# Banded-attention scores as two 64-row matmuls on the two halves of the partitions

## The chip, the cores and the metric

The kernel runs on one core of one Trainium2 chip. The metric is the device time of one execution in microseconds (us), as the median of several runs. The engines carry their usual names in the profile: PE is TensorE (the matrix engine), PEld its loading of weights, DVE is VectorE, ACT is ScalarE, POOL is GpSimd, SP is the engine that issues the transfers.

## The reference

Two layers of a hybrid decoder trunk on 256 tokens with 2048 channels. Each layer has a mixer (three groups of heads side by side: gated linear attention, banded attention with sinks, a short convolution), a cross-attention into 256 memory tokens, and a gated feed-forward part. The part that the change touches is the banded attention: 16 query heads of 64 channels share 2 key heads, a query sees the 128 last positions, and the tokens are cut into two blocks of 128:

```python
def swa_with_sinks(q, k, v, sinks):
    B, T, Hq, hd = q.shape
    ...
    kk, vv = with_prev(k), with_prev(vf)
    s = jnp.einsum('bnqhgd,bnkhd->bnhgqk', qb, kk) * (hd ** -0.5)
    ...
    s = jnp.where(valid[None, :, None, None], s, -jnp.inf)
    ...
    m = jnp.maximum(jnp.max(s, axis=-1, keepdims=True), sink)
    p = jnp.exp(s - m)
    denom = jnp.sum(p, axis=-1, keepdims=True) + jnp.exp(sink - m)
    o = jnp.einsum('bnhgqk,bnkhd->bnqhgd', p / denom, vv)
    return o.reshape(B, T, Hq * hd)
```

The change concerns the first einsum, s.

## The kernel before

All weights are streamed once from memory in pieces of 128 by 1024 (`stream`, L158 to L161): ScalarE casts a piece to the rounded number format fp32r (`wh`), VectorE subtracts to get the rest (`wl`), and every product is made of three matmuls, high by high, high by low and low by high. The large products (`xstat`, L193 to L195, and `wstat`, L176 to L180) give the stream of matmuls; behind each of their steps, `pump` lets one of the waiting tasks go on (the linear attention, the banded attention, the turning of outputs), so that the small matmuls of those tasks stand between the large ones. Three buffers of `wh` and `wl` are in turn. The order of each engine's instructions is not that of the source alone: a scheduler of the framework plans all instructions on a modelled timeline and may move them against each other; `high_priority` moves the weights' casts ahead.

PSUM has eight banks of 512 columns. Four belong to the large products; four are shared by all small products (`self.bank`).

In the banded attention the query heads are stored in pairs: a transposed tile `qT` holds head j of the first key head on partitions 0 to 63 and head j of the second on 64 to 127. `swa_keys` (L597 to L613) turns the rotated keys into `kp`, of shape [128, 2 heads, 2 (high, low), 256]; rows 0 to 63 are filled for head 0 and rows 64 to 127 for head 1, and the other halves are zero (the memset at L600). So one matmul over all 128 rows gives the scores of both heads side by side (L649), one head adding zeros to the other's. `swa` (L634 on) runs for each of two groups g of four head pairs and two blocks n of 128 queries: block 0 has 128 keys (`kw`), block 1 has 256. A bank `sc` holds two head pairs for block 0 and one for block 1; for each pair there are three matmuls (high and low), then one read by VectorE for each head, which adds the mask and takes the maximum (L652), and then the task yields. Over two layers these are 48 score matmuls of 256 columns and 48 of 512.

The early part of a layer that the prediction also speaks of: `zkq` is the projection of the linear attention's keys and queries (wstat), `zq` the one of the banded attention's queries (xstat), `kq` the scaled copy of the first (L714), and `gla` then forms exponents of the gates, `e` and `kd`, on VectorE (L471, L472, L506). L490, L522 and L536 are the linear attention's own products of 64 rows.

Of the kernel before, what the change touches and what calls it, by code (L numbers as in the profile page):

```python
# [9 lines left out]
F32 = mybir.dt.float32  # L10
F32R = mybir.dt.float32r
# [6 lines left out]
P = 128  # L18
D = 2048
T = 256  # L20
# [52 lines left out]
class Trunk:  # L73
# [522 lines left out]

    def swa_keys(self, tok, kp, vp):  # L597

        nc = self.nc
        nc.gpsimd.memset(kp.bitcast(F32), 0.0)  # L600
        nc.gpsimd.memset(vp.bitcast(F32), 0.0)
        kr = self.t512("kr")
        for tb in range(2):
            self.rope(kr[:, tb * P:(tb + 1) * P], tok[tb][:, 16:16 + P], (1.0, -1.0), tb, 2)
        yield W["kr"]
        pk = self.bank("kT")
        for tb in range(2):
            nc.tensor.transpose(out=pk[:, tb * P:(tb + 1) * P], in_=kr[:, tb * P:(tb + 1) * P], identity=self.ident)
        for h in range(2):
            rows, cs = slice(h * 64, h * 64 + 64), slice(h * 64, h * 64 + 64)  # L610
            self.split(kp[rows, h, 0, :], kp[rows, h, 1, :], pk[rows, 0:T])
            for tb in range(2):
                self.split(vp[:, tb, h, 0, cs], vp[:, tb, h, 1, cs], tok[tb][:, 144 + h * 64:208 + h * 64])  # L613

# [19 lines left out]
    def swa(self, g, n, qTs, kp, vp, out):  # L634

        nc = self.nc
        hs = slice(4 * g, 4 * g + 4)
        qT = qTs[n]
        c = self.cols("swc", 32)
        mx, nm, dn, es = (c[:, 8 * i:8 * i + 8].rearrange("p (j h) -> p j h", h=2) for i in range(4))  # L640
        kw = P * (n + 1)
        per = 2 - n
        probs = []
        for j0 in range(0, 4, per):
            sp = self.bank("sc", (P, per, 2, kw))
            pr = self.t512("pr", (P, per, 2, kw))
            for i in range(per):
                for m, (u, v) in enumerate(((0, 0), (0, 1), (1, 0))):
                    nc.tensor.matmul(sp[:, i], lhsT=qT[:, u, j0 + i, :], rhs=kp[:, :, v, 0:kw],  # L649
                                     start=(m == 0), stop=(m == 2))  # L650
                for h in range(2):
                    nc.vector.tensor_tensor_reduce(pr[:, i, h, :], sp[:, i, h, :], self.mask[:, T - kw:T],  # L652
                                                   1.0, -3e38, ALU.add, ALU.max,
                                                   accum_out=mx[:, j0 + i, h:h + 1])
                yield 1
            probs.append(pr)
        nc.vector.scalar_tensor_tensor(nm, mx, -1.0, self.nsink[:, hs, :], ALU.mult, ALU.min)
        nc.vector.tensor_tensor(es, nm, self.nsink[:, hs, :], ALU.subtract)
        for j in range(4):
            for h in range(2):  # L660
                p = probs[j // per][:, j % per, h, :]
                nc.scalar.activation(p, p, AF.Exp, bias=nm[:, j, h:h + 1], accum_out=dn[:, j, h:h + 1])
        nc.scalar.activation(es, es, AF.Exp)
        nc.vector.tensor_tensor(dn, dn, es, ALU.add)
        nc.vector.reciprocal(dn, dn)
        for j in range(4):
            for h in range(2):
                p = probs[j // per][:, j % per, h, :]
                nc.vector.tensor_scalar(p, p, dn[:, j, h:h + 1], None, ALU.mult)
        yield W["p"]  # L670
        ov = self.bank("ov", (P, 4, P))
        parts = [(h, kb) for h in range(2) for kb in range(n + 1)]
        for h, kb in parts:
            pt = self.bank("pT", (P, 4, P))
            for j in range(4):
                nc.tensor.transpose(out=pt[:, j, :], in_=probs[j // per][:, j % per, h, kb * P:(kb + 1) * P],
                                    identity=self.ident)
            pT = self.actp.tile([P, 2, 4, P], F32R, tag="act", name="pT")
            self.split(pT[:, 0], pT[:, 1], pt)
            yield W["pT"]  # L680
            for u, v in ((0, 0), (1, 0), (0, 1)):
                nc.tensor.matmul(ov, lhsT=vp[:, kb, h, u, :], rhs=pT[:, v],
                                 start=((h, kb) == parts[0] and u == v), stop=((h, kb) == parts[-1] and v == 1))
        if not out:
            out += [self.operand(f"ob{2 * g + i}") for i in range(2)]
        for i in range(2):
            ts = slice(n * P, (n + 1) * P)
            self.split(out[i][:, :, 0, ts], out[i][:, :, 1, ts], ov[:, 2 * i:2 * i + 2, :])


    def mixer(self, l, xs, ss, after):
        nc, a = self.nc, self.a
        tok = [self.big(f"tok{tb}", [P, 2 * TOKC]) for tb in range(2)]
        rc, rbc, rt = self.row_factor(ss, "rx", W["ss1"] if l else 1, after)
        pst = self.xstat_both(xs, a["w_tok"][l], name="tokp")
        self.layer_rest(l)
        self.until(rt)
        with self.tc.high_priority(offset=WPRIO):
            for c in range(2):
                for tb in range(2):  # L700
                    nc.scalar.activation(tok[tb][:, c * TOKC:(c + 1) * TOKC], pst[c][tb], AF.Copy,
                                         scale=rc[:, tb:tb + 1])
        qsc = self.par.tile([P, 4], F32, tag="qs", name="qs")
        nc.vector.tensor_scalar(qsc[:, 0:2], rc, 0.125, None, ALU.mult)
        nc.vector.tensor_scalar(qsc[:, 2:4], rc, -0.125, None, ALU.mult)
        fm = lambda g, name: self.fold(self.wstat(xs, a["w_fm"][l, g], name=name), name)
        kq, o_sb = self.big("kq", [P, 2, 512]), self.big("o", [P, 4, T])
        ready = []
        tg = self.start(self.gla(l, tok, kq, ready, o_sb))
        if l == 0:  # L710
            self.rope_tables()
        for g in range(2):
            z = fm(g, "zkq")
            nc.vector.tensor_tensor(kq[:, g, :].rearrange("p (h t) -> p h t", h=2), z,  # L714
                                    rbc.unsqueeze(1).broadcast_to([P, 2, T]), ALU.mult)
        nc.scalar.mul(kq[:, 1, :], kq[:, 1, :], 0.125)
        ready.append(True)
        kp, vp = self.operand("kp"), self.actp.tile([P, 2, 2, 2, P], F32R, tag="act", name="vp")
        tk = self.start(self.swa_keys(tok, kp, vp))
        ob, ts = [], []  # L720
        q = [self.big("q", (P, 2, 512)) for _ in range(2)]
        self.claim(*q)
        for g in range(2):
            qs, qTs = self.swa_rope(q[g], self.xstat(xs, a["w_q"][l, g], name="zq"), qsc), []
            og = []
            ob.append(og)
            tq = self.start(self.swa_queries(qs, qTs))
            ts += [self.start(self.swa(g, n, qTs, kp, vp, og), tk, tq) for n in range(2)]
        if l == 0:
            self.tm = self.start(self.memory_factor())  # L730
        ys, oc = self.big("cy", [P, 4, T]), [self.operand(f"oc{g}") for g in range(2)]
        self.claim(ys, *oc)
        for j in range(4):
            z = fm(4 + j, "zc")
            self.by_row(z, rbc)
            self.conv(j, z[:, 0, :], z[:, 1, :], ys[:, j, :])
        ms = []
        self.start(self.memory(l, ms), *ts)
        for g in range(2):
            z = fm(8 + g, "zb")  # L740
            self.by_row(z, rbc)
            nc.vector.tensor_tensor(z, z, ys[:, 2 * g:2 * g + 2, :], ALU.mult)
            self.split(oc[g][:, :, 0, :], oc[g][:, :, 1, :], z)
        zr, oa = self.big("zr", [P, 2, 2, T]), [self.operand(f"oa{g}") for g in range(2)]
        for g in range(2):
            z = self.fold(self.wstat(xs, a["w_fm"][l, 2 + g], name="zr"), "zr", zr[:, g])
            self.by_row(z, rbc)
        ts.append(self.start(self.gla_out(o_sb, zr, oa), tg, *ts))
        return oc + oa, ob, ts, ms
# [405 lines left out]
```

## Time and profile before

| | us |
|---|---|
| median of 3 runs | 2846.16 (2844.40 to 2846.78) |
| the profiled execution | 2846.51 |
| its span, first to last instruction | 2844.7 |
| TensorE busy | 2825.5 (99%) |
| TensorE's weight loads | 2363.4 (83%) |
| VectorE busy | 1885.5 (66%) |
| ScalarE busy | 1445.7 (51%) |
| GpSimd busy | 15.8 (1%) |

A busy share of TensorE counts overlapping work: a matmul's duration reaches from its start to its modelled end, and the next one starts before that. What a matmul takes of the engine's time is the distance from its start to the next start, as the timeline shows it. A form such as 64\*128 in a row gives the rows and the columns of the array that the matmul uses.

### The profile page before, as it was taken

Reading aid. Unit: us, or ns where it says so; the run is one execution under the profiler, and the core shown is the slowest. Engines: PE = TensorE matmul, PEld = TensorE weight load, DVE = VectorE, ACT = ScalarE, POOL = GpSimd, SP = SyncE. Lnnn points to the kernel's source line nnn. Section 1 sums busy time; section 2 is a strip of 40 time slices with the busy share of each in tenths; the row PEclk is TensorE's granted clock in tenths of the full one; section 3 lists DMA queues with packets and bytes.
Section 4 is the critical chain, followed back from the end, with each engine's and each line's share of the span. In section 5 each row is a group of like instructions: output and inputs, shape, how many; then the busy total and the mean of one; then the engine's idle time right before and its main releaser. Section 6 shows DMA issues by size and latency. Waiting matters only on the chain.

```text
span 2844.7 us, 37041 instructions
## 1 busy us (share of the span) xinstructions
PE 2825.5 (99%) x13554; PEld 2363.4 (83%) x13554; DVE 1885.5 (66%) x2877; ACT 1445.7 (51%) x2060; POOL 15.8 (1%) x44
## 2 busy tenths in 40 slices
PE   9999999999999999999999999999999999999998
PEld 8888888888888888888888888888888888888886
DVE  6886665556777777755567866655567777777445
ACT  7565454445555555544465644544455555555333
POOL 0000000000000000000000000000000000000001
PEclk9999999999999999999999999999999999999999
DMA  6557777557777777766664577775677777777665
GB/s 240 156 175 225 237 243 230 178 171 239 246 239 238 244 242 238 246 209 208 205 194 142 161 227 242 239 221 176 185 238 241 246 245 236 240 242 247 197 193 155
DMA packets 207030, 616.97 MB, mean 217 GB/s; under 512 B 23520, under 2 KB 65024, under 8 KB 206848
## 3 DMA queue, kind: packets, MB, share of 16 engines
q1 hardware_dynamic: 206848, 614.61, 68.9%
q8 instruction: 106, 1.74, 0.3%
q14 instruction: 76, 0.62, 0.1%
HBM read 570.48 MB, written 44.04 MB: 216 GB/s over the span
## 4 chain that ended last, share of the span: by engine, by line
PE 98%; DVE 1%; DMA 1%; ACT 0%; issue 0%; SPq 0%; ACTq 0%
PE up L194 11%; PE up L195 11%; PE up L193 11%; PE fin L821 8%; PE res L195 7%; PE res L193 7%; PE res L194 7%; PE qp L194 2%; PE vp L193 2%; PE vp L195 2%; PE vp L194 2%; PE qp L193 2%; PE qp L195 2%; PE kp L195 2%; PE kp L193 2%; PE kp L194 2%
## 5 line engine op out<-in xcount | busy, mean ns | idle before, releaser
L161 DVE TENSOR_TENSOR wl<-raw,wh 128x1024 fp32r<-128x1024 f32 (+1 forms) x992 | 1201.1, 1212 | 780.3 <-ACT wh L160 778.5
L160 ACT CAST wh<-raw 128x1024 fp32r<-128x1024 f32 (+1 forms) x992 | 1035.5, 1045 | 1140.7 <-PE up L195 329.8
L194 PE MATMUL up<-wl,xs 128*128 128x512 f32 x1408 | 548.1, 389 | 0.0
L193 PE MATMUL up<-wh,xs 128*128 128x512 f32 x1408 | 547.8, 389 | 0.0
L195 PE MATMUL up<-wh,xs 128*128 128x512 f32 x1408 | 547.7, 389 | 0.0
L194 PEld LDWEIGHTS up<-wl,xs 128*128 128x128 f32 x1408 | 264.3, 188 | 55.3 <-DVE wl L161 0.4
L193 PEld LDWEIGHTS up<-wh,xs 128*128 128x128 f32 x1408 | 264.3, 188 | 55.0
L195 PEld LDWEIGHTS up<-wh,xs 128*128 128x128 f32 x1408 | 264.3, 188 | 54.5
L821 PE MATMUL fin<-wh,a 128*128 128x512 f32 x704 | 189.9, 389 | 0.0
L821 PEld LDWEIGHTS fin<-wh,a 128*128 128x128 f32 x704 | 132.2, 188 | 27.5
L193 PE MATMUL res<-wh,a 128*128 128x512 f32 x352 | 136.9, 389 | 0.0
L194 PE MATMUL res<-wl,a 128*128 128x512 f32 x352 | 136.9, 389 | 0.0
L195 PE MATMUL res<-wh,a 128*128 128x512 f32 x352 | 136.9, 389 | 0.0
L1017 ACT ACTIVATE u<-z_t,par 128x256 f32<-128x256 f32 x176 | 91.5, 591 | 36.5 <-DVE z_t L238 36.3
L821 PE MATMUL fin<-wl,a 128*128 128x512 f32 x352 | 110.0, 389 | 0.0
L193 PE MATMUL vp<-wh,ms 128*128 128x512 f32 x256 | 100.3, 392 | 0.0
L193 PE MATMUL qp<-wh,xs 128*128 128x512 f32 x256 | 100.2, 391 | 0.0
L194 PE MATMUL qp<-wl,xs 128*128 128x512 f32 x256 | 100.0, 391 | 0.0
L195 PE MATMUL vp<-wh,ms 128*128 128x512 f32 x256 | 99.9, 390 | 0.0
L194 PE MATMUL vp<-wl,ms 128*128 128x512 f32 x256 | 99.8, 390 | 0.0
L195 PE MATMUL qp<-wh,xs 128*128 128x512 f32 x256 | 99.8, 390 | 0.0
L193 PE MATMUL res<-wh,xo 128*128 128x512 f32 x256 | 99.6, 389 | 0.0
(315 smaller groups left out, 4311.5 us busy)
## 6 DMA issues: line engine op xcount, KB each, us to landing
raw<-in_wu SPq DMA_DIRECT2D x352, 512.0 KB, 4.7
raw<-in_wd SPq DMA_DIRECT2D x176, 512.0 KB, 4.2
raw<-in_w_fm SPq DMA_DIRECT2D x80, 512.0 KB, 4.5
raw<-in_wk SPq DMA_DIRECT2D x64, 512.0 KB, 4.1
raw<-in_wo SPq DMA_DIRECT2D x64, 512.0 KB, 4.3
raw<-in_wq SPq DMA_DIRECT2D x64, 512.0 KB, 4.2
raw<-in_wv SPq DMA_DIRECT2D x64, 512.0 KB, 3.5
raw<-in_wxo SPq DMA_DIRECT2D x64, 512.0 KB, 4.0
```

The source lines that it names most:

```text
L160: nc.scalar.copy(wh[:, :n], raw[:, :n])
L161: nc.vector.tensor_tensor(wl[:, :n], raw[:, :n], wh.bitcast(F32)[:, :n], ALU.subtract)
L193: nc.tensor.matmul(ps[:, tb, :gc], lhsT=xh, rhs=wh, start=(k == 0), stop=False)
L194: nc.tensor.matmul(ps[:, tb, :gc], lhsT=xh, rhs=wl, start=False, stop=False)
L195: nc.tensor.matmul(ps[:, tb, :gc], lhsT=xl, rhs=wh, start=False, stop=(k == kt - 1))
L821: nc.tensor.matmul(ps[c][tb], lhsT=lhs, rhs=w[v][:, c % 2 * 512:c % 2 * 512 + 512], start=(k == 0 and n == 0), stop=(k == FT - 1 and n == 2))
L1017: nc.scalar.activation(u[:, s, :], z[:, s, :], AF.Identity, bias=self.p[:, C_FB + m:C_FB + m + 1], scale=tap[2])
```

## The change

The keys `kp` lose the dimension of heads: they become [128, 2, 256], filled by one cast and one subtraction over all 128 partitions, with no zeroing. Each score matmul becomes two: for h = 0 on partitions 0 to 63 and for h = 1 on partitions 64 to 127, both with half of the columns (128 or 256), each into a bank of its own; a step of `swa` then holds two banks, half filled, instead of one. The reads by VectorE keep their number and size. Below the changed lines the numbers are greater by two.

```diff
 def swa_keys(self, tok, kp, vp):
-        nc.gpsimd.memset(kp.bitcast(F32), 0.0)
         nc.gpsimd.memset(vp.bitcast(F32), 0.0)
...
+        self.split(kp[:, 0, :], kp[:, 1, :], pk[:, 0:T])
         for h in range(2):
-            rows, cs = slice(h * 64, h * 64 + 64), slice(h * 64, h * 64 + 64)
-            self.split(kp[rows, h, 0, :], kp[rows, h, 1, :], pk[rows, 0:T])
+            cs = slice(h * 64, h * 64 + 64)
...
 def swa(self, g, n, qTs, kp, vp, out):
...
-            sp = self.bank("sc", (P, per, 2, kw))
+            sp = [self.bank("sc", (P, per, kw)) for _ in range(2)]
...
                 for m, (u, v) in enumerate(((0, 0), (0, 1), (1, 0))):
-                    nc.tensor.matmul(sp[:, i], lhsT=qT[:, u, j0 + i, :], rhs=kp[:, :, v, 0:kw],
-                                     start=(m == 0), stop=(m == 2))
+                    for h in range(2):
+                        rows = slice(h * 64, h * 64 + 64)
+                        nc.tensor.matmul(sp[h][:, i], lhsT=qT[rows, u, j0 + i, :], rhs=kp[rows, v, 0:kw],
+                                         start=(m == 0), stop=(m == 2))
                 for h in range(2):
-                    nc.vector.tensor_tensor_reduce(pr[:, i, h, :], sp[:, i, h, :], self.mask[:, T - kw:T],
+                    nc.vector.tensor_tensor_reduce(pr[:, i, h, :], sp[h][:, i], self.mask[:, T - kw:T],
...
-        kp, vp = self.operand("kp"), self.actp.tile([P, 2, 2, 2, P], F32R, tag="act", name="vp")
+        kp, vp = self.actp.tile([P, 2, T], F32R, tag="act", name="kp"), self.actp.tile([P, 2, 2, 2, P], F32R, tag="act", name="vp")
```

The scheduler plans the changed program anew. On TensorE, at the first scores of the first layer (sc with two numbers are two banks; here two head pairs of block 0 in each), there stood before:

```order
L195 MATMUL zq_1133<-wh_1296,xs_321 128x512
L649 MATMUL sc_1247<-kp_777,qT_1191 128x256 x3
L193 MATMUL zq_1133<-wh_1296,xs_321 128x512
L649 MATMUL sc_1271<-kp_777,qT_1191 128x256 x3
L194 MATMUL zq_1133<-wl_1297,xs_321 128x512
```

At the same place in the changed program, where 1244 and 1245 are the halves h = 0 and h = 1 of one bank before, and 1275 and 1276 those of the next:

```order
L195 MATMUL zq_1130<-wh_1304,xs_321 128x512
L651 MATMUL sc_1244<-kp_777,qT_1188 128x128 x3
L193 MATMUL zq_1130<-wh_1304,xs_321 128x512
L651 MATMUL sc_1245<-kp_777,qT_1188 128x128 x3
L651 MATMUL sc_1275<-kp_777,qT_1188 128x128
L651 MATMUL sc_1276<-kp_777,qT_1188 128x128
```

The last two rows stand there three times in turn. The three matmuls of h = 0 and the three of h = 1 of the first head pair are apart, with a full-array matmul between them; those of the other bank alternate.

On VectorE, in the early part of the first layer, behind the first kq (wl is the low half of a piece of weights; wl_751 belongs to the last piece of zkq), there stood before:

```order
L161 TENSOR_TENSOR wl_729<-raw_727,wh_728 128x1024
L714 TENSOR_TENSOR kq_529<-zkq_678,rxb_121 128x512
L471 TENSOR_TENSOR e_884<-b_612 128x8x32
L472 TENSOR_TENSOR e_884<-b_612 128x8x32
L506 TENSOR_TENSOR kd_890<-b_612 128x2x192
L471 TENSOR_TENSOR e_884<-b_612 128x16x16
L472 TENSOR_TENSOR e_884<-b_612 128x16x16
L471 TENSOR_TENSOR e_997<-b_612 128x32x8
L472 TENSOR_TENSOR e_997<-b_612 128x32x8
L471 TENSOR_TENSOR e_997<-b_612 128x64x4
L472 TENSOR_TENSOR e_997<-b_612 128x64x4
L161 TENSOR_TENSOR wl_751<-raw_749,wh_750 128x1024
```

In the changed program the same place reads:

```order
L161 TENSOR_TENSOR wl_729<-raw_727,wh_728 128x1024
L716 TENSOR_TENSOR kq_529<-zkq_678,rxb_121 128x512
L161 TENSOR_TENSOR wl_751<-raw_749,wh_750 128x1024
L266 TENSOR_TENSOR vp_778<-tok0_118,vp_778 128x64
L266 TENSOR_TENSOR vp_778<-tok1_119,vp_778 128x64
```

The weights come directly behind kq, and the nine operations on e and kd have moved behind four more pieces of weights. The second layer's order differs in the same way.

## Rows read from the trace of the kernel before

**Rows 1.** The page: span, busy us with share and count, granted clock by slice.

```profile
span 2844.7 us, 37041 instructions
...
PE 2825.5 (99%) x13554; PEld 2363.4 (83%) x13554; DVE 1885.5 (66%) x2877; ACT 1445.7 (51%) x2060; POOL 15.8 (1%) x44
...
PEclk9999999999999999999999999999999999999999
```

**Rows 2.** Waits of TensorE: waiter, waited for, total us, times, longest.

```profile
PE zkq L177 <- DVE wl L161: 2.5, 2, 1.3
PE tokp L211 <- DVE wl L161: 1.5, 4, 0.9
```

**Rows 3.** Windows: length, then busy us and count by engine, clock, DMA share.

```profile
111.00:240.00 129.00, 129.00 (x772) 112.09 (x771) 104.92 (x259) 85.22 (x188) 0.65 (x8) 1.00 0.56 177
```

**Rows 4.** Timeline at score matmuls: start us, length us, engine, line, operation.

```profile
116.58 0.53 PEld L649 LDWEIGHTS sc<-kp,qT 128*128 128x128 f32 x3
116.80 0.52 PE L649 MATMUL sc<-kp,qT 128*128 128x256 f32 x3
...
117.16 0.40 PE L193 MATMUL zq<-wh,xs 128*128 128x512 f32 x1
...
125.07 0.84 PE L649 MATMUL sc<-kp,qT 128*128 128x512 f32 x3
125.75 0.39 PE L193 MATMUL zq<-wh,xs 128*128 128x512 f32 x1
```

**Rows 5.** Timeline at a stretch of 64-row matmuls, L536: matmuls, then weight loads.

```profile
94.46 0.39 PE L193 MATMUL zq<-wh,xs 128*128 128x512 f32 x1
94.78 0.49 PE L536 MATMUL f<-qd,kd 64*128 64x128 f32 x4
95.20 0.50 PE L194 MATMUL zq<-wl,xs 128*128 128x512 f32 x1
...
94.78 0.19 PEld L536 LDWEIGHTS f<-qd,kd 64*128 64x128 f32 x2 [0.35 <-issue]
...
94.89 0.19 PEld L536 LDWEIGHTS f<-qd,kd 64*128 64x128 f32 x2
```

**Rows 6.** Timeline at stretches of 64 by 64 matmuls, L490.

```profile
98.15 0.40 PE L195 MATMUL zq<-wh,xs 128*128 128x512 f32 x1
...
98.47 0.43 PE L490 MATMUL a<-e 64*64 64x32 f32 x16
...
98.84 0.50 PE L193 MATMUL zq<-wh,xs 128*128 128x512 f32 x1
...
99.18 0.40 PE L194 MATMUL zq<-wl,xs 128*128 128x512 f32 x1
...
112.41 0.67 PE L490 MATMUL a<-e 64*64 64x32 f32 x32
113.00 0.50 PE L195 MATMUL zq<-wh,xs 128*128 128x512 f32 x1
```

**Rows 7.** Timeline of three engines at the end of zkq in the first layer.

```profile
65.99 1.04 ACT L160 CAST wh<-raw 128x1024 fp32r<-128x1024 f32 x1
...
69.07 0.39 PE L176 MATMUL zkq<-xs,wh 128*128 128x512 f32 x1
...
69.55 0.50 PE L193 MATMUL zq<-wh,xs 128*128 128x512 f32 x1
...
70.03 1.22 DVE L161 TENSOR_TENSOR wl<-raw,wh 128x1024 fp32r<-128x1024 f32 x1
...
71.31 0.39 PE L177 MATMUL zkq<-xs,wl 128*128 128x256 f32 x1 [1.25 <-DVE wl L161]
...
71.53 0.39 PE L176 MATMUL zkq<-xs,wh 128*128 128x512 f32 x1
```

**Rows 8.** Timeline of TensorE at the same place in the second layer.

```profile
1479.35 0.39 PE L176 MATMUL zkq<-xs,wh 128*128 128x512 f32 x1
...
1481.58 0.39 PE L177 MATMUL zkq<-xs,wl 128*128 128x256 f32 x1 [1.26 <-DVE wl L161]
```

## The prediction

> **What bounds the kernel now.** I read the page first: TensorE is busy for 99% of the span, and its granted clock stands in the highest tenth in every slice, so the higher of its two levels, 2.4 GHz, holds throughout [rows 1]. The waits come next: what TensorE waits for is found only near the start of each layer, where the low halves of the weights come late from VectorE; no matmul of the scores (L649) waits [rows 2]. In the window table TensorE is busy for 129.00 of the 129 us in which the first layer's attention runs [rows 3]. So in the stretches that the change touches, every tenth of a microsecond that TensorE's row of work gains or loses goes straight into the end, and what the other engines gain is hidden. Therefore I priced TensorE's instructions by the distance from one start to the next in the timeline; the durations overlap and can't be added.
>
> In the full-array form (128\*128) three score matmuls of 256 columns move the next matmul from 116.80 to 117.16, which is 0.12 us each, and three of 512 columns from 125.07 to 125.75, which is 0.227 each [rows 4]. That is also the pace of the stream around them, and the weights of each are loaded while its forerunner runs: the loads of the first score group begin at 116.58, 0.22 ahead of its first matmul. The kernel has 48 score matmuls of each width: 48 × 0.12 + 48 × 0.227 = **16.6 us** in all. Even if the halved work cost nothing extra, the most that could be won is some 8 us of 2846.
>
> **The change, part by part.**
>
> *Leaving the full array.* The new score matmuls have 64 rows. The kernel already has stretches of such a form. At 94.46 a full-array matmul starts; the four matmuls of L536 (64\*128, pairs on the two halves) follow 0.32 later and not 0.227; the next full-array matmul comes 0.42 after that [rows 5]. After a return the second full-array matmul comes 0.34 later, as behind the 64\*64 stretch at 98.84 [rows 6]. So a visit of two pairs costs 0.09 + 0.42 + 0.11 = 0.63 us beyond the stream. In it the second pair of loads begins 0.11 after the first pair, both loads of a pair at once [rows 5]: a pair is a step of 0.11, two are 0.22, and **0.41 us** is left for each visit: both changes of form wait until the array is empty, and on either side one weight load is in the open. The 64\*64 stretches say the same: 16 and 32 matmuls take 0.37 and 0.59 [rows 6], so 0.014 a matmul; 0.09 + 0.37 + 0.11 less 16 × 0.014 is 0.35, with shorter loads. Those are the bounds, 0.35 and 0.41; I take 0.41, from the row of the same form. The Trainium skill, "TensorEngine Tiling (Array Packing)", section Tiling Modes, Key Properties, says that a change of the tiling mode drains TensorE; it gives no price, and the trace agrees, with 0.32 for 0.227 ahead of L536 and 0.42 behind it.
>
> How many visits there are is read from the order that the scheduler made. In the changed kernel the scores stand in 40 stretches (20 with 128 columns, 20 with 256), each with full-array matmuls ahead of it and behind it; before there were none, since the scores had the full form. 40 × 0.41 = **+16.4 us**. The older 64-row stretches go from 20 entries out of the full array to 18, since they are grouped otherwise: **−0.8 us**.
>
> *The matmuls themselves.* The source issues them as h = 0, h = 1, h = 0, and so on, but the scheduler mostly puts three of one half, then three of the other, often with a full-array matmul between them (first pair of fences). If a pair standing side by side counts as one step, the 96 matmuls of 128 columns make 78 steps and the 96 of 256 columns make 76, where perfect pairs would make 48 and 48. A step of 256 columns costs 0.12, as the full-array row of that width. No row has 128 columns in the number format of the scores (fp32r); the bounds are half of the 256-column price, 0.06, and the 0.11 at which the weight loads of L536 follow each other. I take 0.11, since each matmul still loads 128 columns of weights. 78 × 0.11 + 76 × 0.12 = 17.7, against 16.6 before: **+1.1 us** (−2.8 with 0.06).
>
> *The order elsewhere.* Dropping the zeroing of the keys and turning four key splits into two moves the scheduler's plan early in both layers. In the kernel before, VectorE does nine operations on the gate exponents before the low weights that TensorE needs (second pair of fences): TensorE's last zkq matmul starts at 69.07, one zq at 69.55, and the next zkq only at 71.31, with a load in the open (0.22 to its successor, where 0.12 is usual) [rows 7]. Continuous work would have started it at 69.07 + 0.23 + 0.23 = 69.53; with 0.10 for the open load the loss is 1.9. The second layer repeats it, 1479.35 to 1481.58 [rows 8]. In the changed order these weights come right behind kq; ScalarE's cast that they need began at 65.99 and took 1.04, so they would be done near 68.3, ahead of the need at 69.3. Two stalls gone: **−3.8 us**, or 0 if the nine operations, now later, hold up another tile of weights. Four further subtractions of weights stand ahead of them in the changed order, so I take the full gain.
>
> *What costs nothing.* The zeroing on GpSimd, and two of four key casts and subtractions, lie under TensorE's work. The reads of the scores by VectorE keep their number and size. Two banks instead of one hold a step's scores, out of four; the matmuls of the second head pair waited for the read of the first before, too, and behind each wait stand the next weights' matmuls. I see no stall there, as there was none [rows 2]; one weight subtraction (1.22 us, the row at 70.03 in [rows 7]) ahead of such a read, once in each of the eight blocks of scores, would cost 9.8.
>
> **The sum.** 16.4 − 0.8 + 1.1 − 3.8 = +12.9 us. The profiled execution took 2846.51, 1.8 beyond its span of 2844.7, and lies 0.35 above the median of 2846.16. So 2859.4 by that execution, and **2859** by the median. The forecast's own range: 0.35 for a visit and a last 128-column step of half length in each of 20 stretches give +9.5 (2856); a stall that doesn't go gives +16.7 (2863).
>
> **The rivals.**
>
> *Faster: pairs at no charge for the change of form.* If a visit cost nothing and a 128-column step 0.06, the sum would be 13.8 − 16.6 − 3.8 = −6.6, so 2839.5. For it: the loads of a pair do start together [rows 5]. Against it: 0.32 and 0.34 where 0.227 is usual, at every visit in [rows 5, 6]. It decides below about 0.02 us a visit. I give it 0.07. The Trainium skill, "TensorEngine Tiling (Array Packing)", section Theoretical Speedup, promises up to twice the speed for at most 64 rows; that would be this case.
>
> *No change: a visit costs about 0.15.* That is so if only one of the two changes of form were paid, or the loads were hidden: 6 + 1.1 − 3.8 = +3.3, 2849.5. The rows at both ends speak against it. 0.12.
>
> *The change doesn't do what it says.* If the halves never run side by side, 96 × 0.11 + 96 × 0.12 = 22.1: +5.5 in place of +1.1, 2863.5. Against it speak the paired starts [rows 5]. 0.10.
>
> *Heavier.* If in a stretch the next weights of the same half waited for the running matmul, the 154 − 40 = 114 later steps would each cost 0.11 more: +12.5, 2872. Against it: the second loads of L536 begin while the first pair runs [rows 5]. Or the banks cost their 9.8: 2869. Together 0.09.
>
> **How the numbers follow.** My forecast has 0.62. A measurement of this kernel can tell some 0.2%, 5.7 us, from no change. Slower: 0.62 + 0.10 + 0.09 = 0.81; same 0.12; faster 0.07. The range of 2848 to 2867 holds the forecast, the unpaired case, most of the no-change case and the lower part of the heavier one; about 0.18 is left out.
>
> **What would show it.** In the profile after, the timeline should show 0.32 from the last full-array matmul to a score stretch and 0.34 behind the first one after it; the groups should show 192 score matmuls of the form 64\*128; TensorE's wait for the zkq low weights should be gone; the attention's part of each layer should be some 8 us longer and its beginning 2 us shorter. I am wrong if the next full-array matmul's weights load while scores still run, if TensorE waits for VectorE's reads of the scores, or if the 128-column steps are much longer than 0.11.

## The result and the profile after

The changed kernel takes 2871.16 us (median of 4 runs, 2867.84 to 2874.07) beside 2845.95 of the kernel before (2844.4 to 2846.78): a ratio of 1.0088, 95% interval 1.0076 to 1.0100, or +25.2 us. The forecast was 2859, the range 2848 to 2867: the sign was right, the size was half of what came, and the time lies outside the range. The profiled execution took 2867.84, 1.7 beyond its span, and is the shortest of the four; against the profiled execution before (2846.51) it is 21.3 longer.

The page still shows a TensorE that hardly pauses; compare [rows 1]:

```profile
span 2866.1 us, 37214 instructions
...
PE 2842.8 (99%) x13650; PEld 2368.7 (83%) x13650; DVE 1889.3 (66%) x2875; ACT 1444.9 (50%) x2058; POOL 13.9 (0%) x42
...
PEclk9999999999999999999999999999999999999999
```

TensorE's waits (waiter, waited for, total us, times, longest) have changed. The zkq wait of [rows 2] is gone, as forecast. Two others are new, at the very end of the attention, in zr, and the forecast has nothing of them:

```profile
PE zr L176 <- ACT wh L160: 5.2, 3, 2.4
PE zr L177 <- DVE wl L161: 2.6, 4, 0.8
```

The visits of the score matmuls look as forecast. Timeline of TensorE (start us, length us, engine, line, operation):

```profile
114.37 0.39 PE L195 MATMUL zq<-wh,xs 128*128 128x512 f32 x1
114.69 0.55 PE L651 MATMUL sc<-kp,qT 64*128 64x128 f32 x3
115.16 0.50 PE L193 MATMUL zq<-wh,xs 128*128 128x512 f32 x1
115.60 0.88 PE L651 MATMUL sc<-kp,qT 64*128 64x128 f32 x9
116.41 0.50 PE L194 MATMUL zq<-wl,xs 128*128 128x512 f32 x1
116.75 0.39 PE L195 MATMUL zq<-wh,xs 128*128 128x512 f32 x1
```

0.32 from the last full-array matmul to the scores and 0.34 from the first one behind them to the next, where 0.227 is usual. But at the end of zr (same columns; in brackets what the engine waited for) this is new:

```profile
236.75 0.85 PE L684 MATMUL ov<-pT,vp 128*128 128x512 f32 x3
239.78 0.49 PE L176 MATMUL zr<-xs,wh 128*128 128x512 f32 x1 [2.18 <-ACT wh L160]
241.04 0.39 PE L177 MATMUL zr<-xs,wl 128*128 128x256 f32 x1 [0.76 <-DVE wl L161]
...
242.27 0.63 PE L176 MATMUL zr<-xs,wh 128*128 128x512 f32 x1
...
242.91 0.63 PE L176 MATMUL zr<-xs,wh 128*128 128x512 f32 x1
...
245.14 0.28 PE L177 MATMUL zr<-xs,wl 128*128 128x256 f32 x1
```

A pair of zr matmuls (512 and 256 columns) takes 0.64 here, from 242.27 to 242.91, and 0.35 elsewhere. The windows of the same stretch (length, busy us and count by engine, then the granted clock, DMA share, GB/s) say why:

```profile
237.00:241.00 4.00, 1.10 (x4) 0.35 (x2) 3.55 (x8) 3.48 (x8) 0.00 (x0) 1.00 0.76 224
...
243.00:245.00 2.00, 2.00 (x8) 1.71 (x8) 1.64 (x3) 1.32 (x2) 0.00 (x0) 0.50 0.73 260
245.00:248.00 3.00, 3.00 (x19) 2.61 (x18) 1.67 (x4) 0.97 (x3) 0.00 (x0) 1.00 0.84 266
```

TensorE was busy for 1.10 of 4 us, and then the granted clock fell to 0.50, the lower level of 1.2 GHz, until 245 (window after it: 1.00). Without the stall the matmul at 245.14 would have come at 236.75 + 3 × 0.227 + 7 × 0.35 + 0.23 = 240.1: 5.0 us are lost. The second layer has the same, from 1656.85 to 1665.08, with six pairs in it in place of seven: 8.23 − 3.01 = 5.2. The first layer has a smaller stall at 250.69 (2.0 by its starts, no fall of the clock), and the second layer a last one at 1671.10 (0.6). Together **12.8 us**.

What ScalarE did ahead of it (its timeline):

```profile
233.14 0.59 ACT L265 CAST pT<-pT 128x512 fp32r<-128x512 f32 x1 [0.49 <-PE pT L678]
233.62 4.51 ACT L278 ACTIVATE ms<-mem,par 128x256 fp32r<-128x256 f32 x11
...
238.29 0.51 ACT L278 ACTIVATE ms<-mem,par 128x256 fp32r<-128x256 f32 x1
238.70 1.03 ACT L160 CAST wh<-raw 128x1024 fp32r<-128x1024 f32 x1
```

The last cast of the attention's probabilities (pT) is followed by 12 casts of memory tokens (ms), and only then comes the cast of the weights for which TensorE waits. In the kernel before the layer's 16 casts of memory tokens came in three lots of 8, 4 and 4, and the last pT cast stood 27 us earlier. The two lines are the summaries of the pT casts (count, length in ns, first and last start), of before and of after:

```profile
L265 ACT CAST pT<-pT x12: 562/586/594, 138.6 to 205.7; 128x512 fp32r<-128x512 f32 x12
```

```profile
L265 ACT CAST pT<-pT x12: 563/588/602, 154.0 to 233.1; 128x512 fp32r<-128x512 f32 x12
```

SyncE's timeline has the other half of it. The memory tokens land in the pool of four buffers in which the weights land too. Their loads went out long before the burst:

```profile
173.93 0.33 SPq L891 DMA_DIRECT2D mem<-in_mem  x1
...
199.57 0.33 SPq L891 DMA_DIRECT2D mem<-in_mem  x1
...
224.82 0.33 SPq L891 DMA_DIRECT2D mem<-in_mem  x1
...
227.21 0.33 SPq L158 DMA_DIRECT2D raw<-in_w_fm  x1
...
233.94 0.33 SPq L158 DMA_DIRECT2D raw<-in_w_fm  x1
```

From 224.82 on three of the four buffers hold memory tokens that nobody has read yet; between 227.21 and 233.94 no load of weights goes out.

**Theory**: the scores now occupy two of four PSUM banks for each step, so their steps spread out and end late; the memory tokens, which are prepared behind them, are late as well, hold the weight buffers and crowd ScalarE, and zr starves. The rest is the forecast's sum. **Rivals**: the visits cost more than the rows say and the stall is an accident of one execution; or the stall comes with the 64-row form; or the doubled number of score matmuls makes them late.

### The profile page after: what moved, and what is told of

Its sections match the earlier page's. It is cut to its first block, busy times and chain, and to the rows that moved or that the text cites. A ratio compares the mean times of both kernels' runs of the same rounds, so it can differ in the third digit from the quotient of the medians.

```text
span 2866.1 us, 37214 instructions
## 1 busy us (share of the span) xinstructions
PE 2842.8 (99%) x13650; PEld 2368.7 (83%) x13650; DVE 1889.3 (66%) x2875; ACT 1444.9 (50%) x2058; POOL 13.9 (0%) x42
## 3 DMA queue, kind: packets, MB, share of 16 engines
q8 instruction: 107, 1.75, 0.3%
## 4 chain that ended last, share of the span: by engine, by line
PE 97%; ACT 1%; DMA 1%; DVE 1%; issue 0%; SPq 0%; ACTq 0%
PE up L194 11%; PE up L193 11%; PE up L195 11%; PE fin L823 8%; PE res L195 7%; PE res L194 7%; PE res L193 7%; PE vp L193 2%; PE vp L194 2%; PE qp L194 2%; PE qp L195 2%; PE vp L195 2%; PE qp L193 2%; PE kp L193 2%; PE kp L195 2%; PE kp L194 2%
## 5 line engine op out<-in xcount | busy, mean ns | idle before, releaser
L195 PE MATMUL up<-wh,xs 128*128 128x512 f32 x1408 | 547.8, 389 | 0.0
L195 PEld LDWEIGHTS up<-wh,xs 128*128 128x128 f32 x1408 | 264.3, 188 | 54.6
L195 PE MATMUL res<-wh,a 128*128 128x512 f32 x352 | 136.9, 389 | 0.0
L195 PE MATMUL vp<-wh,ms 128*128 128x512 f32 x256 | 99.8, 390 | 0.0
L195 PE MATMUL qp<-wh,xs 128*128 128x512 f32 x256 | 99.8, 390 | 0.0
```

What stands on the lines that cost most here:

```text
L195: nc.tensor.matmul(ps[:, tb, :gc], lhsT=xl, rhs=wh, start=False, stop=(k == kt - 1))
```

## The experiments

Times are medians beside the kernel before on the same chip (2845.7 to 2846.3).

**Two banks, full form.** Each score matmul has 128 rows against keys with zero halves, and a bank for each half:

```diff
-            sp = self.bank("sc", (P, per, 2, kw))
+            sp = [self.bank("sc", (P, per, kw)) for _ in range(2)]
...
-                    nc.tensor.matmul(sp[:, i], lhsT=qT[:, u, j0 + i, :], rhs=kp[:, :, v, 0:kw],
-                                     start=(m == 0), stop=(m == 2))
+                    for h in range(2):
+                        nc.tensor.matmul(sp[h][:, i], lhsT=qT[:, u, j0 + i, :], rhs=kp[:, h, v, 0:kw],
+                                         start=(m == 0), stop=(m == 2))
...
```

> The banks, the row of work and the order of the changed kernel, but each score matmul in the full form: 128 rows, against the zeroed other half of the keys, so no change of form and no pairs (96 matmuls of 128 columns, 96 of 256). Theory (the loss is 40 visits at 0.41 = 16.4 us, and a stall in zr of some 5 us a layer that comes from the later order, less 3.8 for the zkq stall): the visits go, the zr stall stays. 96 x 0.11 + 96 x 0.12 = 22.1 against 16.6, -3.8, -0.8 (the older 64-row stretches), +10: 2846 + 10.9 = 2857, with TensorE waiting for ScalarE's wh at the end of zr in both layers and the granted clock falling behind it. Rival (the whole loss hangs on the 64-row form, the zr stall too): 2846 + 5.5 - 4.6 = 2847, no wait in zr.

Measured: 2864.61 (2861.05 to 2866.32), ratio 1.0065 [1.0048, 1.0082]. The stall is there without one 64-row score matmul:

```profile
PE zr L176 <- ACT wh L160: 6.0, 3, 2.1
PE zkq L177 <- DVE wl L161: 2.5, 2, 1.3
PE zr L177 <- DVE wl L161: 2.5, 4, 0.8
```

So the form isn't its cause. The 2857 was too low, first for a reason that the rows show: I had counted the zkq gain of 3.8 as part of the new order, and the zkq wait stays here, since this kernel prepares its keys as before. That gain belongs to the keys. With it left out the expectation is 2861. The profile has three stalls in zr, which by their starts lose some 13 us where the expectation counted 10, with one lower stretch of the clock in each layer; and the older 64-row stretches, for which it took off 0.8, are entered 20 times here, as in the kernel before. Together that makes up the rest.

**The changed kernel again.**

> The changed kernel once more, beside the others. Theory: 2868 to 2874, with the stall at the end of zr in both layers, 3 us of wait in each and the clock at its lower level behind it for some 3 us; what differs from run to run is the length of that stall or of the low clock. Rival: the stall is an accident of the one profiled execution, and another profile shows none; then the time is lost in the score stretches.

Measured: 2869.41 (2867.22 to 2874.13). The profile shows both stalls again, and the smaller one (a wait of 0.64 for wh at 1670.31) now in the second layer, not in the first.

The stall is no accident, and its size differs from execution to execution. Both profiled executions were the shortest of their four; what the longer ones lose was not seen.

**Memory tokens out of the weights' buffers.** One line of the changed kernel:

```diff
-            raw = self.raw.tile([P, 2, 2, T], F32, tag="raw", name="mem")
+            raw = self.big("mem", (P, 2, 2, T))
```

> The changed kernel, with one line altered: the memory tokens land in tiles of the activation pool and no longer take two of the four buffers in which the weights land. Theory: the stall in zr comes from the memory tokens, which are prepared in one burst of 11 or 12 casts ahead of the cast of the zr weights and keep weight buffers occupied until then; in this order the bursts are 8, 3, 1 and 4, and the weights have their four buffers. So no wait for wh or wl in zr, no fall of the clock: 2871 - 10 = 2861. Rival (the stall is made by the score matmuls' banks, or is not worth 10 us): 2868 or more.

Measured: 2858.27 (2856.71 to 2858.91), ratio 1.0045 [1.0030, 1.0060], 11 us under the changed kernel beside it. The scores stand in the same 40 stretches. In the waits of TensorE zr is gone; what is left ahead of kp is small:

```profile
PE kp L193 <- ACT wh L160: 0.9, 1, 0.9
PE kp L194 <- DVE wl L161: 0.6, 1, 0.6
```

This kernel is the forecast's: it has all that the sum of +12.9 holds and no stall, and it takes 2858 where 2859 was forecast. That they agree so well is in part luck, since the visits turn out 2 us cheaper (below) and the waits ahead of kp are not in the sum. The edit also moved the burst: 8 of the casts of memory tokens now stand behind the cast of weights (238.01). So this run alone doesn't tell the occupied buffers from the burst.

**The price of a visit by itself.** The kernel before with probes in the first layer's FFN, whose results nobody reads:

```diff
...
+    PROBES = (None, (64, 1, 128), (64, 3, 128), (64, 3, 256), (128, 1, 128), (128, 4, 128), (64, -3, 128))
+
+    def probe(self, kind, x, w):
+        rows, n, cols = kind
+        halves = list(range(128 // rows))
+        for h in halves * n if n > 0 else sorted(halves * -n):
+            r = slice(h * rows, h * rows + rows)
+            self.tc.keep_in_program_order(self.nc.tensor.matmul(
+                self.spare[h][:, 0:cols], lhsT=x[r], rhs=w[r, 0:cols], start=True, stop=True))
...
```

> The kernel before, with extra matmuls in the first layer's FFN that nothing reads: behind each third matmul of the up projection a visit, 96 visits in each group of three tiles. Tiles 0-2 none; 3-5 one pair of 64-row matmuls of 128 columns on the two halves, two banks; 6-8 three pairs; 9-11 three pairs of 256 columns; 12-14 one full-array matmul of 128 columns; 15-17 four of these; 18-20 three matmuls of one half, then three of the other; 21 none. Theory by the prediction's terms (0.41 a visit, a step 0.11 or 0.12): a pair 0.52 (50 us for the 96), three pairs 0.74 (71), three pairs of 256 0.77 (74), a full matmul 0.11 (11), four 0.44 (42), three and three 0.41 + 5 steps = 0.96 (92). Rival, heavier: weights of the same half wait for the running matmul, so each further step costs 0.22 and more, three pairs 0.96 or more. Rival, lighter: a visit below 0.35.

Measured: 3154.68 (one run), 309.0 above the kernel before. A probe stands behind every third full-array matmul; the distance from one L195 to the next is 0.68 without a probe (704.92 to 705.60). One pair, then three pairs of 128 columns, then three of one half followed by three of the other (timeline of TensorE):

```profile
774.61 0.40 PE L195 MATMUL up<-wh,xs 128*128 128x512 f32 x1
774.93 0.33 PE L208 MATMUL probe<-wh,xs 64*128 64x128 f32 x2
...
775.76 0.40 PE L195 MATMUL up<-wh,xs 128*128 128x512 f32 x1
...
905.43 0.40 PE L195 MATMUL up<-wh,xs 128*128 128x512 f32 x1
905.76 0.55 PE L208 MATMUL probe<-wh,xs 64*128 64x128 f32 x6
906.24 0.50 PE L193 MATMUL up<-wh,xs 128*128 128x512 f32 x1
...
906.81 0.40 PE L195 MATMUL up<-wh,xs 128*128 128x512 f32 x1
...
1436.52 0.40 PE L195 MATMUL up<-wh,xs 128*128 128x512 f32 x1
1436.84 0.56 PE L208 MATMUL probe<-wh,xs 64*128 64x128 f32 x6
...
1437.89 0.39 PE L195 MATMUL up<-wh,xs 128*128 128x512 f32 x1
```

The length of a tile, first matmul to first matmul, gives the mean over the 32 visits in it; a tile without probes is 21.76 us:

| visit | tile, us | cost of one | expected |
|---|---|---|---|
| one pair, 128 columns | 36.91 | 0.47 | 0.52 |
| three pairs, 128 | 43.95 | 0.69 | 0.74 |
| three pairs, 256 | 46.40 | 0.77 | 0.77 |
| three of one half, then three of the other, 128 | 44.11 | 0.70 | 0.96 |
| one full-array matmul, 128 | 25.81 | 0.13 | 0.11 |
| four full-array matmuls, 128 | 36.48 | 0.46 | 0.44 |

The six prices, 96 visits each, add up to 309.2, so they account for the 309.0. A further pair of 128 columns costs (0.69 − 0.47) / 2 = 0.11, so 0.36 is left for the visit (0.41 was forecast); a step of 256 columns is (0.77 − 0.36) / 3 = 0.136. The last expectation fell: three and three cost what three pairs cost, so the order within a visit doesn't matter. That a pair is one step and not two short ones is shown by the changed kernel: its three matmuls of one half alone, at 114.69, last 0.55 and let the next full-array matmul in after 0.47, like the six at 905.76 (0.55 and 0.48).

With these prices the 40 stretches come out as 13 of three and 2 of six matmuls of 128 columns at 0.69, 5 of nine at 0.36 + 6 × 0.11 = 1.02 (the row at 115.60 shows it), and 20 of 256 columns at 0.77: 10.4 + 5.1 + 15.4 = 30.9 us, against 16.6 before, **+14.3**. (A stretch of nine counts as six steps, since its third lot of three is of a half that already had three.)

**Two banks, full form, memory tokens moved.** Both edits above in one kernel.

> Two banks and full-array score matmuls (96 of 128 columns, 96 of 256), with the memory tokens in tiles of the activation pool. Theory: two banks alone cost nothing beyond their extra matmuls once the stall in zr is gone. By the price run a full matmul of 128 columns is 0.127, one of 256 is 0.12: 96 x 0.127 + 96 x 0.12 = 23.7 against 16.6, less 0.8 for the older 64-row stretches, zkq stall as in the kernel before (it stayed in the two-bank kernel): +6.3, so 2852, no wait in zr. Rival (the banks themselves cost, by waits for VectorE's reads): 2857 or more. The distance to the halved kernel with the same memory tiles (2858) is then the price of the 64-row form: by the price run 40 visits x 0.363 + steps 75 x 0.11 + 60 x 0.136 = 30.9 against 23.7, less 3.8 for the zkq stall: +3.4 by theory, so 2855 to 2858 against 2852.

Measured: 2856.33 (2853.89 to 2858.89), ratio 1.0038 [1.0024, 1.0052]. No wait in zr; 4 us more than expected, of which the profile shows some 3 as waits that the kernel before doesn't have (up for wl 1.4, kp for wh 0.9 and for wl 0.5). Another 0.8 had been taken off for the older 64-row stretches, which are entered 20 times here, as before.

The changed kernel with the memory tokens moved takes only 2 us more. By the prices it is 3.4: 30.9 − 23.7 = 7.2 for the 64-row form, less 3.8 for the zkq wait, which only that kernel loses. The intervals overlap, so the sign of the difference is not shown by this pair.

**One bank, halves in full form.** What makes the scores late: the second bank, or that there are twice as many matmuls?

```diff
-                for m, (u, v) in enumerate(((0, 0), (0, 1), (1, 0))):
-                    nc.tensor.matmul(sp[:, i], lhsT=qT[:, u, j0 + i, :], rhs=kp[:, :, v, 0:kw],
-                                     start=(m == 0), stop=(m == 2))
+                for h in range(2):
+                    for m, (u, v) in enumerate(((0, 0), (0, 1), (1, 0))):
+                        nc.tensor.matmul(sp[:, i, h], lhsT=qT[:, u, j0 + i, :], rhs=kp[:, h, v, 0:kw],
+                                         start=(m == 0), stop=(m == 2))
```

> The kernel before, with each score matmul cut in two by key half (192 full-array matmuls, 96 of 128 columns and 96 of 256), but both halves of a step in one bank, as before. Memory tiles in the weight buffers, as before. Theory (the second bank of a step, not the number or the form of its matmuls, makes the scores late and so the memory tokens): the last pT cast of the first layer stays near 206 us, where two banks had it at 231; no stall in zr; 96 x 0.127 + 96 x 0.12 = 23.7 against 16.6: +7.1, 2853. Rival (the doubled number of matmuls delays the scores): the last pT cast near 231, a wait for wh at the end of zr, 2860 or more.

Measured: 2855.33 (2852.75 to 2858.19), ratio 1.0034 [1.0022, 1.0046]; the profiled execution is 8.2 longer than the one before, where the matmuls alone make 7.1. The pT casts end where they ended before, and there is no wait in zr:

```profile
L265 ACT CAST pT<-pT x12: 560/585/618, 138.8 to 204.9; 128x512 fp32r<-128x512 f32 x12
```

With two banks a step and matmuls of the same form and number it was:

```profile
L265 ACT CAST pT<-pT x12: 564/587/605, 155.6 to 231.3; 128x512 fp32r<-128x512 f32 x12
```

So it is the second bank of a step that makes the scores late, not their number. (The two kernels also differ in that the halves stand one after the other here and alternate there; no run changes that order alone.) The Trainium skill, "TensorEngine Tiling (Array Packing)", Gotcha 1: PSUM Pressure, says that row tiling raises the demand for PSUM, since different row tiles write to different banks. The traces agree: with two banks a step the last pT cast is at 233.1 (64-row form) or 231.3 (full form), with one at 205.7 or 204.9.

**Two weight buffers held, nothing else.** In the kernel before, from the zb projections until zr's first result:

```diff
+        held = [self.raw.tile([P, 1024], F32, tag="raw", name="held") for _ in range(2)]
+        for t in held:
+            nc.vector.memset(t[:, 0:16], 0.0)
...
+        for t in held:
+            nc.vector.tensor_tensor(t[:, 0:16], t[:, 0:16], zr[:, 0, 0, 0:16], ALU.add)
```

> The kernel before, with two of the four buffers in which weights land kept occupied from zb until the first zr result; nothing else is held up, scores as before in one bank and the full form. Theory (the zr stall is made by memory tiles that occupy weight buffers): with two buffers fewer the loads of the zb and zr weights come late, TensorE waits for wh in zb or zr some us in each layer and its granted clock falls to 0.50 behind the wait: 2852 to 2866. Rival (the stall is made by the burst of memory casts ahead of the weights' cast on ScalarE): 2846 to 2848, no wait beyond 1 us.

Measured: 2860.86 (2859.18 to 2861.34), ratio 1.0053 [1.0039, 1.0066]. The same picture in zr, and the clock behind it (windows, columns as above):

```profile
231.13 0.51 PE L176 MATMUL zr<-xs,wh 128*128 128x512 f32 x1 [1.42 <-ACT wh L160]
232.39 0.38 PE L177 MATMUL zr<-xs,wl 128*128 128x256 f32 x1 [0.75 <-DVE wl L161]
```

```profile
229.50:233.60 4.10, 1.93 (x10) 1.27 (x9) 1.23 (x1) 1.47 (x2) 0.00 (x0) 1.00 0.40 126
233.60:237.00 3.40, 3.40 (x13) 2.92 (x12) 1.23 (x1) 1.20 (x2) 0.00 (x0) 0.50 0.53 169
```

Occupied buffers are enough for such a stall: ScalarE had two instructions in the 4.1 us around it (1.47 us), so no burst stood there, and the cast of the weights in question, at 230.03, had itself waited 1.75 for its load. Waits of 3.5 us ahead of kp are part of the loss, too. In the changed kernel both causes can be at work, since the cast at 238.70 stood behind the burst and its load had gone out late. The load of 233.94 tells how they share (SyncE's transfers; the last number is from its issue to its landing in us):

```profile
raw<-in_w_fm SPq DMA_DIRECT2D x1, 512.0 KB, 4.0
```

It landed at about 237.9, so at most 0.8 of TensorE's 2.18 us can be the burst's, and the late load sets the rest. In the second layer the load goes out at 1653.80 and takes 3.9, and the cast comes at 1658.99: at most 1.3 of 2.37.

**The zkq stall alone, in the kernel before.**

```diff
-            nc.vector.tensor_tensor(e3[:, :, 0:hs], ref, b3[:, :, 0:hs], ALU.subtract)
+            first = nc.vector.tensor_tensor(e3[:, :, 0:hs], ref, b3[:, :, 0:hs], ALU.subtract)
+            if lv < 2:
+                self.tc.keep_in_program_order(first)
```

> The kernel before, with the first operation on the gate exponents of levels 0 and 1 kept behind what was issued ahead of it on VectorE, so that the low half of the zkq weights stands ahead of most of the nine operations. Theory (these operations were the whole cause of the zkq stall): TensorE's wait of 2.5 for the zkq low weights goes, -1.9 a layer: 2842. Rival (the stall has another cause, the cast or the load): 2846, the wait stays. Second rival: the operations now stand ahead of other weights and stall them: 2846 or more, a new wait.

Measured: 2840.66 (2839.21 to 2842.18), ratio 0.9982 [0.9973, 0.9991]. VectorE's timeline has the low weights two operations behind kq, where nine stood between them before, and TensorE no longer waits there:

```profile
65.87 0.68 DVE L716 TENSOR_TENSOR kq<-zkq,rxb 128x512 f32<-128x512 f32 x1
66.48 0.75 DVE L474 TENSOR_TENSOR e<-b 128x256 f32<-128x256 f32 x2
67.15 1.22 DVE L161 TENSOR_TENSOR wl<-raw,wh 128x1024 fp32r<-128x1024 f32 x1
```

That is 5.7 us by the medians and 5.0 by the profiled executions, where 3.8 was expected, although one new wait of 1.6 us for wh stands in the second layer's zr. The order of other work changed with it (the scores stand in 28 stretches and no longer in 30). The older 64-row stretches are entered 16 times where the kernel before has 20, some 1.4 us by the 0.36 of a visit (an estimate); what the rest is made of is open.

**Both repairs, scores as before.**

> Scores as in the kernel before, with both repairs: the first operation on the gate exponents of levels 0 and 1 kept back on VectorE, and the memory tokens in tiles of the activation pool. Theory: the one wait that the repair of zkq left, 1.6 us for wh in the second layer's zr, comes from weight buffers that memory tiles occupy, so it goes: 2839. Rival: the four memory loads now come together near the end of zr and delay the first kp weights, as in both kernels with this edit (a gap of 1.4 us ahead of kp in the first layer, 0.9 in the second): 2841 or more.

Measured: 2839.94 (2838.44 to 2842.43), ratio 0.9979 [0.9970, 0.9989]: faster than both kernels. Of the wait in zr 0.4 us is left, and kp doesn't wait. Over the kernel with the zkq repair alone it is no gain that the runs can tell (ranges 2839.21 to 2842.18 and 2838.44 to 2842.43).

## Why the prediction was wrong, and which of its terms held

*Leaving the full array* (+16.4): right in mechanism, some 2 us too high. 40 visits at 0.36 are 14.4. The 0.41 came from a single visit of L536, whose operands are f32 and not fp32r.

*The matmuls themselves* (+1.1): the result fits and the count was wrong. I took 78 and 76 steps, as if three of one half and then three of the other were six steps; the probes show that they are three. That leaves 75 and 60. But a step of 256 columns takes 0.136 and not 0.12. 75 × 0.11 + 60 × 0.136 = 16.4, or −0.2 against 16.6. The bound of half-length 128-column steps (0.06) is out: 0.11 holds.

*The order elsewhere* (−3.8): right. The wait is gone in the changed kernel, it stays in both two-bank kernels that prepare the keys as before, and moving the operations alone removes it, too. The older stretches (−0.8) are entered 18 times, as counted, but what that saves was not measured by itself.

*What costs nothing*: here the prediction failed, at "I see no stall there". I asked whether TensorE would wait for VectorE's reads of the scores, found that it wouldn't, and it doesn't. I didn't ask what comes later when a step takes two banks of four: the steps spread out by 27 us, and the memory tokens, which are prepared behind the scores, move from a place with room to the last weights of zr. The term was 0 and measured 12.8 us in the profiled execution: 14.3 − 0.8 − 3.8 + 12.8 = 22.5, where 21.3 was measured; which term is 1.2 too high is not shown. Without the stall the sum is +9.7 by the corrected terms; the kernel with moved memory tokens has +12.4 by its profiled execution, of which its waits ahead of kp are 1.5; the other 1.2 are open.

*The rivals and the range*: "banks cost their 9.8" had nearly the size of the stall for a wrong reason (reads of the scores, in each block) and, together with the heavier weights, a chance of 0.09. The heavier weights have 2872, the number nearest to the 2871 measured, and that is luck: they want 0.22 for a further step of the same half, and the probes have 0.11. The range ended at 2867, below that rival's 2869, and left out what happened. The faster and the no-change cases fell with the probes: a visit costs 0.36. Six halves of 128 columns, as three pairs, cost 0.69, and six full-array matmuls of that width, by the 0.46 of four, the same. The Trainium skill, "TensorEngine Tiling (Array Packing)", section Theoretical Speedup, has up to twice the speed for at most 64 rows. The steps here have it, with 0.11 for a pair of 128 columns and 0.11 for each further full-array matmul, (0.46 − 0.13) / 3; in visits of three steps the 0.36 takes it back.

## What to carry to other kernels

A matmul that uses half of the rows saves nothing where it interrupts a stream in the full form for a few steps: each interruption costs 0.36 us, as much as three steps. By these prices a pair of 256 columns saves 0.09 against one full-array matmul of 512 (0.136 for 0.227), so some four such steps in a row would pay for a visit, and a pair of 128 columns saves 0.01. That is an estimate; no visit here had more than three steps of 256 columns. When an edit takes a second buffer of a small pool, ask what else is prepared behind the work that will now be late, which buffers that work holds meanwhile, and which engine's queue it will then stand in, even where no wait is visible before. And a wait of 2 to 3 us can cost more than its length: behind most such places here the clock was low for some 3 us.

## What the runs showed of the hardware

Within one visit the order of the two halves is free: three and three of 128 columns (0.70) cost as much as three alternating pairs (0.69).

Whether TensorE's clock falls after a wait isn't told by the wait's length alone. In the changed kernel it fell to 0.50 behind waits of 2.18 and 0.76 us with one matmul between them, and in the kernel with two buffers held behind 1.42 and 0.75. In the two-bank kernel it stayed at 1.00 behind almost the same waits, 2.13 and 0.77 (first row and first window), and fell behind the next, 2.03 and 0.77 (second row and second window):

```profile
237.95 0.49 PE L176 MATMUL zr<-xs,wh 128*128 128x512 f32 x1 [2.13 <-ACT wh L160]
...
249.60 0.49 PE L176 MATMUL zr<-xs,wh 128*128 128x512 f32 x1 [2.03 <-ACT wh L160]
```

```profile
239.50:242.00 2.50, 2.50 (x16) 2.21 (x16) 2.50 (x5) 1.69 (x3) 0.00 (x0) 1.00 0.85 275
...
251.20:254.60 3.40, 3.40 (x13) 2.90 (x12) 2.47 (x3) 0.76 (x1) 0.00 (x0) 0.50 0.84 277
```

What decides it is open.
